# Low parts of 216 split weight blocks: ScalarE negation and an accumulating DMA instead of a VectorE subtraction

## The chip, the cores and the metric

One Trainium2 chip, one of its cores. The metric is the device time of one execution in microseconds (us). The kernel before has a median of 2792.41 us over 3 runs (2788.8 to 2797.22).

## The reference, cut to what matters

One decoder layer over 2048 tokens of 1024 channels, in float32. A conditioning vector gives a shift, a scale and a gate for each of the two halves of the layer:

```
h = rmsnorm(x) * (1 + sc_mix) + sh_mix
proj = h @ w_in                       # 1024 x 4624, split into z, xbc, dt, glu_a, glu_b
y = gated_rmsnorm(ssd_chunked(silu(causal_dwconv(xbc, 4 taps)), dt) + skip, z)
u = silu(layernorm(causal_dwconv(glu_a * sigmoid(glu_b), 31 taps)))
x = x + g_mix * (concat(y, u) @ w_out)             # 2048 x 1024
h = rmsnorm(x) * (1 + sc_mlp) + sh_mlp
x = x + g_mlp * (square(relu(h @ w_mlp1)) @ w_mlp2)
out = rmsnorm(x)
```

## The kernel before, in words

Channels lie on the 128 partitions, tokens on the free axis. The sequence is worked in two halves of 1024 tokens, each as two quarters (`qq`) of 512, which is the width of one matmul's result.

**Two-part operands.** A float32 product is made from two reduced-precision parts of each operand: the high part is a copy in the type float32r, the low part is the raw value minus the high part. Of a product three matmuls are made: high weight with high activation, high weight with low activation, low weight with high activation. For each slice `k` of a weight block they stand in this order (lines 303, 304 and 305 in the input projection, 846 to 848 in the output projection, 1085 to 1087 in the second MLP product), so the low part of a block is first wanted by its third matmul.

**Weight blocks.** `split_w` (line 288) fetches one block of 128 x 1024 float32 (512 KB): SyncE issues the load into `wr` (line 290, a ring of 3 buffers, shared with the loads of `m_d`, of `w1` and of `hid_d`), ScalarE copies it to the high part `wh` (line 293, a ring of 2), VectorE subtracts to make the low part `wl` (line 294, a ring of 2). These two run under `urgent()`, which gives them the first priority when the order of each engine's instructions is laid down. `split_w` is called 216 times: 72 blocks of the input projection (`w_in`), 64 of the output projection (`w_out`), 80 of the second MLP product (`w2`). Eight of the calls name their own destination (`big` buffers), the first four of these at the very start; 208 use `wh` and `wl`.

**How long one block serves.** In the input projection a block serves both quarters: 2 x 8 slices x 3 = 48 matmuls. In `mix_q` (output projection, called four times, 16 blocks each) a block serves one quarter: 24 matmuls. In `down` (second MLP product, called twice) the first three of four rounds use 48 matmuls a block (line 1117, 2 x 24 blocks), the last round 24 (line 1136, 2 x 16 blocks).

**Order of the stages in the span:** input projection with the SSD chunks, half 0 (0 to about 520 us) and half 1 (to about 1018); output projection of half 0 (1018 to about 1195); first MLP product of half 0 (`up`, to about 1530, which uses `w1` and not `split_w`); `down` of half 0 (to about 2030), whose last round is interleaved by blocks with the output projection of half 1 (to about 2100); `up` of half 1 (to about 2390); `down` of half 1 (to the end).

**Work beside it.** VectorE also makes the 31-tap convolution (`conv_cf`, lines 368 to 391: gather of `u_d` into `cu`, some 45 steps a tile, stores to `v_d`), put far back in priority, so that it fills gaps. The convolution of half 1 runs from about 1050 us. The layer norm over it (`ln_cf`, lines 400 to 429) gathers `v_d` into `cu`, sums with a matmul (line 410) and stores to `m_d`. In the input projection each of 12 convolution blocks a half (`conv_ssd`) has two small GpSimd copies a quarter (`halo`, lines 656 and 658) between ScalarE's evacuation (657) and VectorE's taps (662).

**GpSimd's queue.** GpSimd executes in order and issues these transfers: loads of `w_ada` (177), `u_d` (354, 368, 390 and 391 for `v_d`), 400 and 429 of the layer norm, stores of `x2_d` (920, each behind the evacuation 851), stores of `hid_d` (1059, behind ScalarE's line 1004) and loads of `hid_d` (1076, 64 of them, into the `wr` ring). The order on every engine's queue is laid down when the kernel is built.

The lines that hold the split:

```python
        raw = t_wr()
        nc.sync.dma_start(raw, src)
        hi, lo = dst or (t_turn("wh", 2, [P, D], F32R), t_turn("wl", 2, [P, D], F32R))
        with urgent():
            A.activation(hi, raw, AF.Copy)
            V.tensor_tensor(lo, raw, f(hi), SUB)
```

Of the kernel before, what the change touches and what calls it, by code (L numbers as in the profile page):

```python
# [9 lines left out]
F32R = mybir.dt.float32r  # L10
AF = mybir.ActivationFunctionType
ALU = mybir.AluOpType
MULT, ADD, SUB, MAX, MIN = ALU.mult, ALU.add, ALU.subtract, ALU.max, ALU.min

P = 128
S = 2048
D = 1024
# [29 lines left out]
def tile_layer(ctx, tc, x, w_ada, w_mod, vecs, w_in, w_dt, w_out, w1, w2, out):  # L47
    nc = tc.nc
    V, A, G, T = nc.vector, nc.scalar, nc.gpsimd, nc.tensor
# [12 lines left out]
    def nm(s):  # L62
        count[0] += 1
        return f"{s}{count[0]}"
# [4 lines left out]
    def t_turn(tag, n, shape, dt=F32):  # L69
        i = turns.get(tag, 0)  # L70
        turns[tag] = i + 1
        return cp.tile(shape, dt, tag=f"{tag}{i % n}", name=nm(f"{tag}{i % n}_"))
# [66 lines left out]
    @contextmanager  # L139
    def urgent():  # L140
        a = tc.cur_priority
        tc.cur_priority = 0
        yield
        tc.cur_priority = a + 1

    def f(ap):
        return ap.bitcast(F32)
# [137 lines left out]
    def t_wr():  # L285
        return t_turn("wr", 3, [P, D])

    def split_w(src, dst=None):
        raw = t_wr()
        nc.sync.dma_start(raw, src)  # L290
        hi, lo = dst or (t_turn("wh", 2, [P, D], F32R), t_turn("wl", 2, [P, D], F32R))
        with urgent():
            A.activation(hi, raw, AF.Copy)  # L293
            V.tensor_tensor(lo, raw, f(hi), SUB)  # L294
        return hi, lo


# [196 lines left out]
    for half in range(2):  # L494
        pre = {}
        if half == 0:
# [5 lines left out]
            for sg in range(4):  # L502
                wts.append([d_wm().rearrange("p (a b) -> p a b", a=2) for _ in range(4)])
                for j in range(4):
                    nc.sync.dma_start(wts[sg][j], w_mod[sg, j])
                held[W0[sg]] = split_w(w_in[W0[sg]], (d_bx(F32R), d_bx(F32R)))
# [54 lines left out]
            for n, b in enumerate(W1):  # L561
                held[b] = split_w(w_in[b])
                pre[b] = [t_mm()]
                block_mm(pre[b][0], held[b], hq0)
                if n == 0:
                    rs1 = bcast(rs1)
                    hq1 = []
                    for k in range(KT):
                        V.tensor_tensor(x1[k], x1[k], rs1, MULT)
                        hq1.append(lead_h(x1[k], k, d_hq[1](F32R)))  # L570
            hq = [hq0, hq1]
        else:
            held = {b: split_w(w_in[b]) for b in W0[:2]}
            hq = [hq0]
            pre["dt"] = [t_bm()]
# [656 lines left out]
```

## Time and profile before

| what | value |
|---|---|
| median of 3 runs | 2792.41 us (2788.8 to 2797.22) |
| the profiled execution, its own time | 2800.03 us |
| its span, first to last instruction | 2798.2 us |
| mean granted TensorE clock | 0.981 |
| bytes moved | 367.94 MB, mean 131 GB/s |

PE is TensorE's matmul side, PEld its weight load, DVE is VectorE, ACT is ScalarE, POOL is GpSimd, SP is SyncE; a q behind a name is the engine's instruction queue. Matmuls are pipelined, so the 0.39 us of one matmul row overlaps the next one's; the distance from start to start is what a matmul costs. A line number is that of the kernel's file.

### The profile page before, as it was taken

The page shows a single profiled execution, that of the slowest core. Times are in us where ns is not written, and L with a number is a line of the kernel's source. Part 1 is how long each engine was busy: PE and PEld are TensorE (multiplying, and loading weights), DVE is VectorE, ACT ScalarE, POOL GpSimd, SP SyncE. Part 2 cuts the span into 40 slices and gives each one's busy share as a digit, 9 for nine tenths or more (in the row PEclk, how much of TensorE's full clock was granted, in tenths as well). Part 3 has the DMA queues.
Part 4 walks back from the last instruction along what each step waited for, and adds up shares of the span by engine and source line. Part 5 has one row for each costly group of instructions (what it writes and reads, how often), then busy time and mean ns, then how long its engine had stood idle before and what let it go on. Part 6 is the DMA issues. An engine that isn't in the chain of part 4 may idle for free. (4 is left out here: it accounts for less than half of the span.)

```text
span 2798.2 us, 33574 instructions
## 1 busy us (share of the span) xinstructions
PE 2699.3 (96%) x12652; PEld 2195.9 (78%) x12652; DVE 2005.0 (72%) x3024; ACT 1360.2 (49%) x2065; POOL 273.3 (10%) x421
## 2 busy tenths in 40 slices
PE   7999999999999999979999899999998999999998
PEld 5778878788887788857887787888886888788886
DVE  7889999989986669999999755355457444433335
ACT  4757445586745664455565333242336555511222
POOL 2320210030030000000111110000000000100000
PEclk9999999999999999989999999999998999999999
DMA  7463224223223456413435543346632323623322
GB/s 286 141 197 114 84 85 134 77 92 111 85 91 106 136 189 214 140 61 128 142 129 176 179 144 121 97 146 208 203 116 87 113 98 121 223 91 100 106 83 106
DMA packets 115556, 367.94 MB, mean 131 GB/s; under 512 B 13376, under 2 KB 22208, under 8 KB 115392
## 3 DMA queue, kind: packets, MB, share of 16 engines
q1 hardware_dynamic: 79552, 239.54, 25.6%
q0 software_dynamic: 35840, 126.24, 13.3%
q8 instruction: 99, 1.62, 0.2%
q14 instruction: 65, 0.53, 0.1%
HBM read 281.58 MB, written 84.15 MB: 131 GB/s over the span
## 5 line engine op out<-in xcount | busy, mean ns | idle before, releaser
L293 ACT ACTIVATE wh<-wr 128x1024 fp32r<-128x1024 f32 x208 | 219.6, 1056 | 518.4 <-PE mm L1086 297.2
L303 PE MATMUL mm<-big,wh 128*128 128x512 f32 x1024 | 413.0, 403 | 4.1 <-DVE tp L708 3.6
L305 PE MATMUL mm<-big,wl 128*128 128x512 f32 x1024 | 404.4, 395 | 0.0
L1085 PE MATMUL mm<-big,wh 128*128 128x512 f32 x1024 | 401.9, 392 | 1.1 <-ACT wh L293 1.1
L304 PE MATMUL mm<-big,wh 128*128 128x512 f32 x1024 | 401.3, 392 | 0.0
L1087 PE MATMUL mm<-big,wl 128*128 128x512 f32 x1024 | 400.7, 392 | 0.6 <-DVE wl L294 0.5
L1086 PE MATMUL mm<-big,wh 128*128 128x512 f32 x1024 | 400.0, 391 | 0.0
L294 DVE TENSOR_TENSOR wl<-wr,wh 128x1024 fp32r<-128x1024 f32 x208 | 254.0, 1221 | 82.1 <-ACT wh L293 68.5
L1091 DVE SCALAR_TENSOR_TENSOR tp<-mm,gate,tp 128x512 f32<-128x512 f32 x128 | 95.3, 749 | 226.7 <-PE mm L1087 226.3
L303 PEld LDWEIGHTS mm<-big,wh 128*128 128x128 f32 x1024 | 193.1, 189 | 54.0 <-issue 9.2
L305 PEld LDWEIGHTS mm<-big,wl 128*128 128x128 f32 x1024 | 192.7, 188 | 43.8 <-issue 3.2
L304 PEld LDWEIGHTS mm<-big,wh 128*128 128x128 f32 x1024 | 193.2, 189 | 43.1 <-issue 4.7
L1087 PEld LDWEIGHTS mm<-big,wl 128*128 128x128 f32 x1024 | 193.2, 189 | 42.0 <-DVE wl L294 1.4
L1085 PEld LDWEIGHTS mm<-big,wh 128*128 128x128 f32 x1024 | 193.3, 189 | 41.6 <-ACT wh L293 1.9
L1086 PEld LDWEIGHTS mm<-big,wh 128*128 128x128 f32 x1024 | 193.2, 189 | 40.0
L848 PE MATMUL mm<-big,wl 128*128 128x512 f32 x512 | 199.8, 390 | 0.7 <-DVE wl L294 0.5
L846 PE MATMUL mm<-big,wh 128*128 128x512 f32 x512 | 200.0, 391 | 0.4 <-ACT wh L293 0.4
L847 PE MATMUL mm<-big,wh 128*128 128x512 f32 x512 | 199.3, 389 | 0.0
L383 DVE SCALAR_TENSOR_TENSOR ca<-cu,vec,ca 128x512 f32<-128x512 f32 x240 | 178.7, 744 | 1.1 <-ACT ca L377 0.9
L386 DVE SCALAR_TENSOR_TENSOR ca<-ca,hsum,ca 128x512 f32<-128x512 f32 x240 | 178.5, 744 | 0.0
L385 DVE SCALAR_TENSOR_TENSOR ca<-cu,vec,ca 128x513 f32<-128x513 f32 x224 | 167.4, 747 | 6.1 <-ACT ca L379 6.0
L878 DVE TENSOR_TENSOR big<-wr,big 128x1024 fp32r<-128x1024 f32 x64 | 77.7, 1222 | 120.3 <-ACT big L877 120.1
(281 smaller groups left out, 5289.9 us busy)
## 6 DMA issues: line engine op xcount, KB each, us to landing
wr<-in_w_dram SPq DMA_DIRECT2D x144, 512.0 KB, 3.4
wr<-in_w_in_dram SPq DMA_DIRECT2D x72, 512.0 KB, 3.5
wr<-in_w_out_dram SPq DMA_DIRECT2D x64, 512.0 KB, 4.1
hid_d<-tp POOLq DMA_DIRECT2D x64, 512.0 KB, 3.8
wr<-hid_d POOLq DMA_DIRECT2D x64, 512.0 KB, 3.9
ca<-in_w_ada_dram POOLq DMA_DIRECT2D x64, 256.0 KB, 3.6
tp<-ac_d SPq DMA_DIRECT2D x32, 512.0 KB, 4.3
wr<-m_d SPq DMA_DIRECT2D x32, 512.0 KB, 4.1
```

The costliest lines, as they stand in the source:

```text
L293: A.activation(hi, raw, AF.Copy)
L294: V.tensor_tensor(lo, raw, f(hi), SUB)
L303: T.matmul(ps, lhsT=hi[:, c], rhs=a[:, 0, :], start=(k == 0), stop=False)
L304: T.matmul(ps, lhsT=hi[:, c], rhs=a[:, 1, :], start=False, stop=False)
L305: T.matmul(ps, lhsT=lo[:, c], rhs=a[:, 0, :], start=False, stop=(k == KT - 1))
L383: V.scalar_tensor_tensor(a, x0[:, HP - i : HP - i + L], w(30 - 2 * i), a, MULT, ADD)
L846: T.matmul(ps, lhsT=hi[:, c], rhs=a[:, 0, :], start=(pos + k == 0), stop=False)
L847: T.matmul(ps, lhsT=hi[:, c], rhs=a[:, 1, :], start=False, stop=False)
L848: T.matmul(ps, lhsT=lo[:, c], rhs=a[:, 0, :], start=False, stop=(pos == 1 and k == KT - 1))
L1085: T.matmul(ps, lhsT=whl[0][:, c], rhs=hi, start=(k == 0), stop=False)
L1086: T.matmul(ps, lhsT=whl[0][:, c], rhs=lo, start=False, stop=False)
L1087: T.matmul(ps, lhsT=whl[1][:, c], rhs=hi, start=False, stop=(k == FB - 1))
```

## The change

The low part's buffer first gets minus the high part, by ScalarE; then GpSimd issues a DMA that reads the raw weights from device memory a second time and adds them to what lies in the buffer. The `wl` ring goes from 2 to 3 buffers. VectorE has no part in `split_w` any more. The line is in `split_w`, so that all 216 calls get it.

```diff
         raw = t_wr()
         nc.sync.dma_start(raw, src)
-        hi, lo = dst or (t_turn("wh", 2, [P, D], F32R), t_turn("wl", 2, [P, D], F32R))
+        hi, lo = dst or (t_turn("wh", 2, [P, D], F32R), t_turn("wl", 3, [P, D], F32R))
         with urgent():
             A.activation(hi, raw, AF.Copy)
-            V.tensor_tensor(lo, raw, f(hi), SUB)
+            A.activation(lo, f(hi), AF.Copy, scale=-1.0)
+            nc.gpsimd.dma_start(lo, src, accum_op=ADD)
         return hi, lo
```

## Rows read from the trace of the kernel before

**Rows 1.** The page: busy time of the engines; ScalarE's copy and VectorE's subtraction.
```profile
PE 2699.3 (96%) x12652; PEld 2195.9 (78%) x12652; DVE 2005.0 (72%) x3024; ACT 1360.2 (49%) x2065; POOL 273.3 (10%) x421
L293 ACT ACTIVATE wh<-wr 128x1024 fp32r<-128x1024 f32 x208 | 219.6, 1056 | 518.4 <-PE mm L1086 297.2
L294 DVE TENSOR_TENSOR wl<-wr,wh 128x1024 fp32r<-128x1024 f32 x208 | 254.0, 1221 | 82.1 <-ACT wh L293 68.5
```

**Rows 2.** Waits of PE (two) and ACT: total us, times, longest.
```profile
PE mm L1087 <- DVE wl L294: 0.5, 1, 0.5
PE mm L848 <- DVE wl L294: 0.5, 1, 0.5
ACT wh L293 <- PE mm L1086: 297.2, 55, 19.7
ACT wh L293 <- PE mm L847: 114.7, 36, 5.1
```

**Rows 3.** Busy time by stage: PE, PEld, DVE, ACT, POOL, clock, DMA share, GB/s.
```profile
1200.00:1300.00 100.00, 79.33 (x308) 60.10 (x307) 93.36 (x150) 55.17 (x96) 6.11 (x11) 0.85 0.26 90
1400.00:1500.00 100.00, 99.43 (x439) 81.97 (x438) 99.48 (x153) 57.68 (x98) 8.22 (x14) 1.00 0.35 119
1900.00:2000.00 100.00, 100.00 (x451) 83.08 (x450) 54.85 (x74) 34.58 (x46) 3.27 (x6) 1.00 0.71 235
10.00:45.00 35.00, 26.79 (x92) 14.64 (x91) 28.14 (x54) 14.70 (x23) 2.41 (x5) 0.90 1.03 407
```

**Rows 4.** Timeline, output projection of half 1: start, length, [idle before <- releaser].
```profile
2064.19 1.06 ACT L293 ACTIVATE wh<-wr 128x1024 fp32r<-128x1024 f32 x1 [4.33 <-PE mm L847]
2069.63 1.06 ACT L293 ACTIVATE wh<-wr 128x1024 fp32r<-128x1024 f32 x1 [4.38 <-PE mm L847]
```

**Rows 5.** Timeline, long blocks of `down`: ScalarE's copy, matmuls at a block boundary.
```profile
2648.91 1.06 ACT L293 ACTIVATE wh<-wr 128x1024 fp32r<-128x1024 f32 x1 [3.42 <-PE mm L1086]
2648.94 0.39 PE L1085 MATMUL mm<-big,wh 128*128 128x512 f32 x1
...
2649.39 0.39 PE L1087 MATMUL mm<-big,wl 128*128 128x512 f32 x1
...
2659.79 1.06 ACT L293 ACTIVATE wh<-wr 128x1024 fp32r<-128x1024 f32 x1 [9.82 <-PE mm L1086]
```

**Rows 6.** Timeline of `up`: two dependent ScalarE steps, the GpSimd store behind them.
```profile
2250.89 0.63 ACT L1003 ACTIVATE tp<-sp 128x512 f32<-128x512 f32 x1
2251.55 0.63 ACT L1004 ACTIVATE tp<-tp 128x512 f32<-128x512 f32 x1
2252.48 0.53 POOL L1059 DMA_DIRECT2D hid_d<-tp  x1 [16.03 <-ACT tp L1004]
```

**Rows 7.** GpSimd's 512 KB loads of line 1076: issue length, time from issue to landing.
```profile
L1076 POOL DMA_DIRECT2D wr<-hid_d x64: 528/528/554, 1492.8 to 2662.4; - x64
DMA to landing us min/median/max: 3.7/3.9/10.6
```

**Rows 8.** GpSimd's waits in the input projection, on VectorE: total us, times, longest.
```profile
POOL up L656 <- DVE big L662: 73.8, 24, 13.6
```

**Rows 9.** The chain that ended last, around 1590 us: start, length, what.
```profile
1584.09 0.77 DMA v_d<-ca
1587.80 3.94 DMA cu<-v_d
1593.70 1.22 PE bm L410 x2
```

**Rows 10.** One window of VectorE's line 294 alone: length, busy (count), clock, DMA.
```profile
1050.00:1584.00 534.00, 36.54 (x30) 0.97 0.44 147
```

**Rows 11.** Windows of PE alone: length, PE busy (matmuls), clock, DMA share, GB/s.
```profile
1205.00:1245.00 40.00, 23.19 (x73) 0.66 0.09 33
2100.00:2130.00 30.00, 18.60 (x57) 0.66 0.12 39
1584.00:1600.00 16.00, 9.16 (x28) 0.68 0.40 131
```

## The prediction

> **What bounds the kernel now.** I read the page's engine totals first: PE is busy 96% of the span, DVE 72%, ACT 49%, POOL 10% [rows 1]. So TensorE is the bound, and taking 254 us of DVE work away is worth only what PE waits for DVE. The list of waits says how much that is: all of PE's direct waits for the low part are 1.0 us [rows 2]. In the table by stage DVE is nearly full only from about 200 to 800 and 1000 to 1580 us, and PE beside it is at 99% in the row at 1400 [rows 3]; the exceptions are a dip at 1205 to 1245 and one at 1584 to 1600, where PE idles and the mean granted clock is 0.66 to 0.68, between its two levels of 1.0 (2.4 GHz) and 0.5 (1.2 GHz) [rows 11].
>
> Then the cycle of one weight block, from the timelines. ACT's copy to the high part almost always waits for PE: 55 and 36 waits, 297 and 115 us, on the last reader of the buffer [rows 2]. With two `wh` buffers, the high part of block n+2 starts when block n ends: 2648.91 against 2648.94 for the first matmul of the next block [rows 5]. A 48-matmul block lasts 10.88 us (2648.91 to 2659.79 [rows 5]); a 24-matmul block 5.44 us (2064.19 to 2069.63 [rows 4]). From that boundary the low part now takes 1.06 us on ACT and 1.22 on DVE [rows 1], 2.3 us, against 5.44 or 10.88 us of matmuls in between. It is covered everywhere.
>
> **The change part by part.**
>
> *DVE's subtraction goes:* 208 x 1.221 = 254 us of DVE [rows 1], plus 8 alike. PE waits 1.0 us for it. What can be won lies in the two dips. At 1584 PE waits for the convolution of half 1: the store lands, the gather takes 3.94 us, three DVE steps, then the sum on PE [rows 9]. From 1584 to 1600 PE ran 28 matmuls [rows 11] where, at 5.44 / 24 = 0.227 us each, 70 fit, so 42 x 0.227 = 10 us are lost. Between 1050 us, where this convolution starts, and 1584 stand 30 of the subtractions, 36.5 us of an almost full DVE [rows 10], so the convolution should end that much earlier and this wait goes. The dip at 1205 has 73 matmuls in 40 us, the same transition at 2100, with no convolution beside it, 57 in 30 us [rows 11]: 176 and 132 fit, so 103 x 0.227 = 23 us are lost against 75 x 0.227 = 17, so 6 us more can be had. Together 0 to -16 us; I take -12, since the order of the queues is laid down anew.
>
> *ACT's negation comes:* 216 x 1.06 = 229 us on an engine at 49% [rows 1], which goes to 57%. It delays the evacuation behind it by 1 us; the five PSUM buffers cover that, and I cost it at 0 (without that cover, 1 us a block).
>
> *The accumulating DMA comes:* 216 transfers of 512 KB, 113 MB more on 368. The new path from block boundary to finished low part is 1.06 (copy) + 0.03 (dependent ACT steps: 2250.89 + 0.63 to 2251.55) + 1.06 (negation) + 0.30 (ACT's end at 2252.18 to the POOL issue at 2252.48 [rows 6]) + D, so L = 2.45 + D, where D is issue to landing. No row shows an accumulating DMA. The nearest is the same size on the same queue without the addition, 3.7 at least, 3.9 median, 10.6 at most [rows 7]. An accumulate must read the buffer too: another 512 KB at the 407 GB/s that the full DMA engines reach [rows 3] is 1.3 us. I take D = 3.9 + 1.3 = 5.2, nearest to the median row, and keep 3.7 and 10.6 as bounds. L is then 7.65 us instead of 2.3.
>
> The Trainium skill, DMA: Bandwidth & Descriptors (section Anatomy of one DMA, the SWDGE path), fits a GpSimd transfer with about 2.0 us plus its bytes at 436 GB/s, an estimate of 3.2 us for 512 KB, by which no short block would stall and the first rival below would hold. The trace does not agree: even the plain copy never lands under 3.7 us [rows 7].
>
> *What that costs on short blocks.* Low n+2 is ready L after the end of block n. Block n+2 stops at its third matmul, 0.45 us in (2648.94 to 2649.39 [rows 5]), until then, and block n+1 fills one period p of that time. So two periods are L - 0.45 + 5.44, and p = (L + 4.99) / 2. A stall appears for L above 5.89 and half the excess is paid per block: (7.65 - 5.89) / 2 = 0.88 us. The 64 blocks of the output projection and 32 of the last rounds of `down` make 96 x 0.88 = +84 us. Bounds: D = 3.7 gives 0.13 x 96 = +12, D = 10.6 gives 3.58 x 96 = +344. A gain is excluded for this term: PE lost 1 us here before.
>
> *On long blocks* the limit is 10.88 + 0.45 = 11.3 us; L leaves 3.7 us. The third `wl` buffer lets ACT write before block n's low part is free, so it costs nothing. But POOL's queue is in order: the new issue waits for ACT, and stands behind `halo` copies that wait for ACT or DVE. Of these, 24 waits on DVE average 3.1 us, just inside the margin, and the longest is 13.6 [rows 8], 9.9 beyond it. I take +8, one such; bounds 0 and 24 x 9.9 = 238. Behind the waiting issue stand `hid_d` loads and `x2_d` stores, wanted many blocks later: 0.
>
> *At the start* the DMA engines are full, 407 GB/s from 10 to 45 us [rows 3]. Six early blocks add 3.1 MB, 7.7 us there; some of the loads are not awaited, so +4 (0 to 8; twice that if the second read counts fully). In 1900 to 2000, at 235 GB/s [rows 3], some 18 short blocks add 94 GB/s, twice that with the buffer's read: 423, slightly too much; the 4 us over are inside the bound of D.
>
> *SP* is relieved: `wr` is free after ACT's copy, 1.2 us earlier. Nothing waits on it more than now: 0.
>
> **Sum:** 84 + 8 + 4 - 12 = +84 us on the profiled execution's 2800.03 gives 2884. That execution is 7.6 above the median of 2792.41 (its span 2798.2 plus 1.8 around it), so 2876 for a median.
>
> **Rivals.**
>
> *Hidden, and DVE's relief counts.* With D near 3.7 the stalls are 12 us, the dips give 16, the rest nothing: 2788, no change. At D of 3.4 or less no stall is left: 2776. It decides at D = 3.8, where 96 x (D - 3.44) / 2 equals 16. For it: the plain copy lands at 3.7 at best. Against it: the median is 3.9 [rows 7], and that without a second read. This is the case on the other side: it is faster through the two dips, and D decides.
>
> *The accumulate is slow.* It may add at a lower rate than it reads, or queue behind other transfers: D = 8 is inside the spread of the plain copies [rows 7]. Then L = 10.45, the stall 2.28 x 96 = 219, and with that in place of the forecast's 84 the time is 3011; at 10.6 it is 3136. At D = 8 PE would idle for 30% of those stages; should the clock fall to half there, a block lasts 10.9 us, and the same L is covered, so the damage has a ceiling.
>
> *POOL's order.* Issues stuck behind instructions that wait for a late DVE, in the input projection: 24 waits beyond the margin by half of 9.9 us, 119 us on top, 2995. For it: POOL does wait there on DVE, 73.8 us in total [rows 8]. Against: behind a wait POOL may have had nothing else to do, the issue is urgent, and a relieved DVE is late less often.
>
> That DVE would not be relieved can't be: the instruction is gone from `split_w`.
>
> **Chances.** Forecast (slower, some 40 to 130 us) 0.50; hidden 0.22, of which faster 0.12 and same 0.10; slow accumulate 0.20; POOL's order 0.08. A measurement of this kernel can tell about 0.3%, 8.4 us, from no change. So faster 0.12, same 0.10, slower 0.78. The range takes in the forecast, most of the hidden case and half of the slow one: 2780 to 3060; the forecast's own is 2830 to 2930.
>
> **What the changed profile would show.** The subtraction's place taken by an ACT row of about 1.06 us, 208 times; DVE near 1750 us; a row of 216 accumulating issues on POOL whose landing time is D: right is 4.5 to 6, wrong below 4 or over 8. In PE's waits, the low-part matmuls of the output projection and of `down` should wait for that DMA by about 0.9 us a block in 1018 to 1195, in 1850 to 2100 and after 2690, and those of the input projection hardly at all. The wait at 1584 should be gone. I am wrong if the short blocks still have a 5.44 us pitch, or if the loss lies in the input projection.

## The result and the profile after

The changed kernel takes 3042.03 us (median of 4 runs, 3040.76 to 3047.01) against 2790.61 us for the kernel before on the same chip (4 runs, 2786.38 to 2797.22): ratio 1.0902, 95% interval 1.0876 to 1.0928, or 251 us slower. The forecast was slower by 84. The profiled execution's span is 3040.6 us, 242.4 longer than before.

The page of the changed kernel, engine totals and the costliest groups; every line behind 294 has moved down by one. [rows 1] and the first two of [rows 2] answer to them.

```profile
PE 2772.7 (91%) x12652; PEld 2228.2 (73%) x12652; DVE 1769.0 (58%) x2808; ACT 1568.7 (52%) x2277; POOL 438.0 (14%) x637
...
PEclk8999999999999989989999999999998999999999
...
L1088 PE MATMUL mm<-big,wl 128*128 128x512 f32 x1024 | 408.0, 399 | 48.6 <-DMA wl<-in_w_dram 48.4
...
L293 ACT ACTIVATE wh<-wr 128x1024 fp32r<-128x1024 f32 x208 | 219.7, 1056 | 621.5 <-PE mm L1087 355.6
L294 ACT ACTIVATE wl<-wh 128x1024 fp32r<-128x1024 f32 x208 | 218.7, 1052 | 2.7
L849 PE MATMUL mm<-big,wl 128*128 128x512 f32 x512 | 217.1, 425 | 95.2 <-DMA wl<-in_w_out_dram 95.1
```

VectorE lost 236 us of work and ScalarE gained 208, about as the parts said. But PE now waits 95.1 and 48.4 us for low parts, where it waited 1.0 [rows 2]. The number of matmuls is the same, yet PE is busy 73 us longer (2772.7 against 2699.3 [rows 1]): the same matmuls run at a lower clock (mean granted clock 0.959 against 0.981). The other 169 us of the longer span are PE's idle time, 3040.6 - 2772.7 = 268 against 2798.2 - 2699.3 = 99.

The accumulating issues of line 295: length of the issue on GpSimd (min/median/max), then the time from issue to landing.

```profile
L295 POOL DMA_DIRECT2D wl<-in_w_dram x80: 835/858/920, 1659.4 to 3013.9; - x80
L295 POOL DMA_DIRECT2D wl<-in_w_in_dram x64: 835/857/963, 67.7 to 1022.7; - x64
L295 POOL DMA_DIRECT2D wl<-in_w_out_dram x64: 835/852/936, 1059.4 to 2291.3; - x64
...
DMA to landing us min/median/max: 5.2/6.5/11.5
```

This is D, the term that no row of before showed: 6.5 us, above the 5.2 taken and inside the bounds of 3.7 and 10.6. The raw loads on SP's queue land nearly as before (medians 3.4 to 4.4 us).

The timeline of the changed kernel in the output projection of half 1, all short blocks: start, length, what, and in brackets the idle time before and its releaser.

```profile
2126.59 1.06 ACT L293 ACTIVATE wh<-wr 128x1024 fp32r<-128x1024 f32 x1 [0.52 <-PE mm L848]
2127.61 0.63 ACT L241 ACTIVATE sp<-tp 128x512 f32<-128x512 f32 x1
2128.14 1.04 ACT L294 ACTIVATE wl<-wh 128x1024 fp32r<-128x1024 f32 x1
...
2129.47 0.84 POOL L295 DMA_DIRECT2D wl<-in_w_out_dram  x1 [0.87 <-ACT wl L294]
...
2126.62 0.39 PE L847 MATMUL mm<-big,wh 128*128 128x512 f32 x1
...
2129.05 0.50 PE L849 MATMUL mm<-big,wl 128*128 128x512 f32 x1 [1.82 <-DMA wl<-in_w_out_dram]
2129.39 0.39 PE L847 MATMUL mm<-big,wh 128*128 128x512 f32 x1
...
2138.02 0.69 PE L849 MATMUL mm<-big,wl 128*128 128x512 f32 x1 [3.22 <-DMA wl<-in_w_out_dram]
2138.51 0.63 PE L847 MATMUL mm<-big,wh 128*128 128x512 f32 x1
2138.93 0.63 PE L848 MATMUL mm<-big,wh 128*128 128x512 f32 x1
...
2141.49 0.44 PE L848 MATMUL mm<-big,wh 128*128 128x512 f32 x1
2141.77 0.40 PE L849 MATMUL mm<-big,wl 128*128 128x512 f32 x1
```

At 2126.6 a high buffer has had its last reader (line 848); the copy starts at once, as in [rows 4]. Then another ScalarE step (line 241, a square) gets in front of the negation, GpSimd issues at 2129.47, and the third matmul that needs this low part starts at 2138.02: 11.4 us from the boundary, 8.5 of them the landing. The block in between had waited too, at 2129.05, for its own low part. After the wait at 2138 the matmuls follow at 0.43 us, nearly twice the 0.227 of [rows 4], from 2138.51 to 2141.49: the granted clock is at the lower of its two levels. Not every wait is followed by such a stretch. Of PE's 73 us more of busy time, 48 lie in the two output projections (22 and 26), which have 46 waits for low parts and, in the trace's clock record, 15 stretches at the lower level.

Windows of the changed kernel: length, busy time of PE, PEld, DVE, ACT, POOL (instructions), granted clock, DMA share, GB/s. They answer to [rows 3]; the first line is the kernel before in its output projection of half 0.

```profile
1019.00:1201.00 182.00, 180.73 (x816) 148.78 (x815) 172.49 (x261) 85.63 (x119) 15.70 (x25) 1.00 0.57 187
...
1100.00:1200.00 100.00, 73.96 (x286) 57.32 (x286) 66.47 (x101) 42.16 (x53) 17.41 (x23) 0.90 0.80 216
...
2100.00:2200.00 100.00, 78.54 (x305) 60.42 (x304) 21.24 (x31) 41.22 (x50) 15.63 (x21) 0.93 0.84 217
...
10.00:45.00 35.00, 22.58 (x65) 10.34 (x64) 21.68 (x45) 15.67 (x23) 3.39 (x6) 0.72 1.03 381
```

In these stretches of the two output projections PE is busy only 74 and 79% of the time, with the clock at 0.90 to 0.93, where it was full at 1.00 before. At the start, with the DMA engines as full as before, PE gets 4 us less done and the clock is 0.72 instead of 0.90.

Where the 242 us lie, by the first matmul of each stage, in us; the columns on the right are experiments told below (short: accumulation only in the 96 short blocks; long: in all others; input: only in the 64 ring blocks of the input projection; plain: all 216 transfers as plain copies; negation: no DMA, VectorE adds). By the lines of the matmuls, the stages follow one another: all of `down` of half 0, its last round of 16 short blocks too, lies before the output projection of half 1 (1549 to 1919 us and 1919 to 2097 in the kernel before), and is not interleaved with it as the kernel's description in words has it (in the changed kernel one block overlaps). The expectations call this output projection the stretch of last round and output projection of half 1.

| stage | before | after | short | long | input | plain | negation |
|---|---|---|---|---|---|---|---|
| input projection | 1019 | 1059 | 1018 | 1053 | 1057 | 1031 | 1017 |
| output projection, half 0 (32 short blocks) | 182 | 261 | 269 | 180 | 183 | 229 | 193 |
| `up`, half 0 | 348 | 339 | 340 | 344 | 343 | 340 | 346 |
| `down`, half 0 (24 long, 16 short) | 370 | 400 | 385 | 375 | 366 | 380 | 367 |
| output projection, half 1 (32 short) | 178 | 246 | 257 | 178 | 178 | 218 | 182 |
| `up`, half 1 | 334 | 333 | 334 | 335 | 334 | 335 | 335 |
| `down`, half 1 (24 long, 16 short) | 368 | 404 | 391 | 379 | 367 | 384 | 368 |

### The profile page after: what moved, and what is told of

Same layout as the page of the kernel before. It is cut to its first block, busy times and chain, and to the rows that moved or that the text cites. A ratio compares the mean times of both kernels' runs of the same rounds, so it can differ in the third digit from the quotient of the medians.

```text
span 3040.6 us, 34112 instructions
## 1 busy us (share of the span) xinstructions
PE 2772.7 (91%) x12652; PEld 2228.2 (73%) x12652; DVE 1769.0 (58%) x2808; ACT 1568.7 (52%) x2277; POOL 438.0 (14%) x637
## 4 chain that ended last, share of the span: by engine, by line
PE 38%; issue 30%; DMA 13%; DVE 10%; ACT 5%; POOL 3%; POOLq 0%; SPq 0%; DVEq 0%; ACTq 0%
PE mm L306 5%; PE mm L304 5%; PE mm L305 5%; PE mm L1031 4%; PE mm L1032 4%; PE mm L1033 3%; DMA wl<-in_w_out_dram 3%; PE mm L1088 2%; PE mm L1086 2%; PE mm L1087 2%; DMA tp<-ac_d 2%; POOL wl L295 2%; DMA wr<-hid_d 1%; DMA cu<-v_d 1%; DVE ca L384 1%
## 5 line engine op out<-in xcount | busy, mean ns | idle before, releaser
L1088 PE MATMUL mm<-big,wl 128*128 128x512 f32 x1024 | 408.0, 399 | 48.6 <-DMA wl<-in_w_dram 48.4
L304 PE MATMUL mm<-big,wh 128*128 128x512 f32 x1024 | 418.4, 409 | 2.3 <-DVE sp L671 2.2
L1086 PE MATMUL mm<-big,wh 128*128 128x512 f32 x1024 | 407.2, 398 | 7.9 <-ACT wh L293 7.9
L306 PE MATMUL mm<-big,wl 128*128 128x512 f32 x1024 | 404.8, 396 | 8.9 <-DMA wl<-in_w_in_dram 8.9
L1087 PE MATMUL mm<-big,wh 128*128 128x512 f32 x1024 | 404.3, 395 | 0.0
L305 PE MATMUL mm<-big,wh 128*128 128x512 f32 x1024 | 404.0, 394 | 0.0
L849 PE MATMUL mm<-big,wl 128*128 128x512 f32 x512 | 217.1, 425 | 95.2 <-DMA wl<-in_w_out_dram 95.1
L1088 PEld LDWEIGHTS mm<-big,wl 128*128 128x128 f32 x1024 | 196.0, 191 | 99.0 <-DMA wl<-in_w_dram 58.4
L306 PEld LDWEIGHTS mm<-big,wl 128*128 128x128 f32 x1024 | 194.8, 190 | 54.1 <-DMA wl<-in_w_in_dram 11.8
L1086 PEld LDWEIGHTS mm<-big,wh 128*128 128x128 f32 x1024 | 196.5, 192 | 49.6 <-ACT wh L293 9.6
L304 PEld LDWEIGHTS mm<-big,wh 128*128 128x128 f32 x1024 | 195.1, 191 | 50.3 <-issue 9.5
L305 PEld LDWEIGHTS mm<-big,wh 128*128 128x128 f32 x1024 | 194.9, 190 | 46.2 <-issue 7.1
L1087 PEld LDWEIGHTS mm<-big,wh 128*128 128x128 f32 x1024 | 196.0, 191 | 41.5
L294 ACT ACTIVATE wl<-wh 128x1024 fp32r<-128x1024 f32 x208 | 218.7, 1052 | 2.7
L847 PE MATMUL mm<-big,wh 128*128 128x512 f32 x512 | 212.3, 415 | 4.3 <-ACT wh L293 4.3
L848 PE MATMUL mm<-big,wh 128*128 128x512 f32 x512 | 210.6, 411 | 0.0
L849 PEld LDWEIGHTS mm<-big,wl 128*128 128x128 f32 x512 | 102.9, 201 | 136.7 <-DMA wl<-in_w_out_dram 115.4
```

What stands on the lines that cost most here:

```text
L294: A.activation(lo, f(hi), AF.Copy, scale=-1.0)
L304: T.matmul(ps, lhsT=hi[:, c], rhs=a[:, 0, :], start=(k == 0), stop=False)
L305: T.matmul(ps, lhsT=hi[:, c], rhs=a[:, 1, :], start=False, stop=False)
L306: T.matmul(ps, lhsT=lo[:, c], rhs=a[:, 0, :], start=False, stop=(k == KT - 1))
L847: T.matmul(ps, lhsT=hi[:, c], rhs=a[:, 0, :], start=(pos + k == 0), stop=False)
L848: T.matmul(ps, lhsT=hi[:, c], rhs=a[:, 1, :], start=False, stop=False)
```

## The experiments

The theory after the result: the chain from block boundary to finished low part is longer than the 5.89 us that a short block has for it (one block of 5.44 us and the 0.45 before the third matmul), mostly by D; half the excess is paid per block; the waits also cost clock. The rest is a smaller loss in the input projection and the long blocks.

**Where: the short blocks undone.** The 96 short blocks get VectorE's subtraction back:

```diff
+            if acc:
                 A.activation(lo, f(hi), AF.Copy, scale=-1.0)
                 nc.gpsimd.dma_start(lo, src, accum_op=ADD)
+            else:
+                V.tensor_tensor(lo, raw, f(hi), SUB)
...
-                        whl = split_w(ws[n])
+                        whl = split_w(ws[n], acc=False)
...
```

> Undoes the change in the 96 blocks that serve 24 matmuls only (64 of the output projection, 32 of the last rounds of the second MLP product): VectorE subtracts there again; the other 120 blocks keep the negation and the accumulating DMA. Theory (the loss is the late low part of short blocks, plus TensorE's clock falling after each such wait): the two output projection stretches go back from 260 and 246 us to 182 and 178, the last round of half 1 gives back some 30, so about 3042 - 78 - 68 - 35 = 2860, and the rest above 2791 lies in the input projection (40 us) and the long rounds. Rival (113 MB more traffic and GpSimd's full queue slow everything): 120 of 216 transfers stay, so over half of the 251 us stays, 2930 or more, and the output projection stretches get back at most half.

Measured 2853.44, ratio 1.0211 (1.0185 to 1.0237). The two output projections are back at 180 and 178 us. The theory holds: most of the loss is theirs. About 62 us are left. Its waits on the low parts of long blocks:

```profile
PE mm L1091 <- DMA wl<-in_w_dram: 13.1, 6, 6.5
```

**The other way round: only the short blocks accumulate** (the same flag, with the opposite values).

> The converse of the first run: the change only in the 96 blocks that serve 24 matmuls, VectorE's subtraction in the other 120. Theory (late low parts of short blocks are most of the loss, and the parts add up): 3042 - 2853 = 189 us of the loss belong to these blocks, so about 2792 + 189 = 2980; the input projection lasts 1019 us again, within 5. Rival (the parts feed one another, the long blocks' transfers delay the short ones'): under 2930.

Measured 2989.63, ratio 1.0709 (1.0688 to 1.0731): 197 us by the short blocks alone (2989.63 - 2792.98), and with the 62 of the run above (2853.44 - 2791.8) a little more than the whole 251. The landing of its accumulating DMAs:

```profile
DMA to landing us min/median/max: 5.1/6.3/10.7
```

And PE's waits on low parts in this run: total, times, longest.

```profile
PE mm L852 <- DMA wl<-in_w_out_dram: 107.3, 41, 6.7
PE mm L1091 <- DMA wl<-in_w_dram: 38.5, 18, 4.5
```

No other transfer makes low parts here, so the two rows are the whole direct wait of the short blocks: 145.8 us. The prediction's formula with D at 6.5 gives (2.45 + 6.5 - 5.89) / 2 x 96 = 147. The median of this run is 6.3, but a sum goes by the mean, which is 6.5 here: 6.8 for the 64 blocks of the output projections and 5.9 for the 32 of `down`. Taken apart, the formula gives 108 and 40 us, the rows show 107.3 and 38.5. PE stands still at about every second block (59 waits in 96 blocks) and then for the whole excess.

In PE's own time the 196 us of longer span are 132 us more idle time (the 145.8, less some other waits that went) and 64 us more busy time for the same matmuls (2763.0 against 2699.3), 59 of these in the two output projections. The first 183 us of the first of them, in this run (the kernel before is the first line of the windows above):

```profile
1018.00:1201.00 183.00, 137.46 (x532) 107.45 (x530) 113.71 (x188) 84.42 (x112) 30.34 (x39) 0.86 0.77 204
```

**How much of D is the addition.** A plain copy in place of the accumulation:

```diff
-            nc.gpsimd.dma_start(lo, src, accum_op=ADD)
+            nc.gpsimd.dma_start(lo, src)
```

> The same DMA without the addition: GpSimd copies the raw weights over the negated high part, so the low part holds the raw weights and the correction is left out of the low part's sum. Same bytes from device memory, same queue, same waits. Theory (issue to landing is 6.5 us because an accumulate reads the buffer, adds and writes): it falls to 3.9 to 4.4, L from about 9.4 to 7.1, the idle time per short block from 1.75 to 0.6 us, the total to 2880 to 2920. Rival (the transfer is late because of its queue and of the DMA engines' load): it stays over 5.5 us and the total over 3000.

Measured 2924.69, ratio 1.0472 (1.0445 to 1.0498), a little above the range given. The landing of the copies:

```profile
DMA to landing us min/median/max: 3.5/4.8/8.8
```

PE's waits on low parts with the plain copy:

```profile
PE mm L849 <- DMA wl<-in_w_out_dram: 55.6, 40, 5.7
PE mm L1088 <- DMA wl<-in_w_dram: 21.8, 23, 2.3
```

So the addition costs 1.7 us of landing, and the same transfer without it already takes 4.8 in these places, not the 3.9 of [rows 7]. The waits follow D: the formula gives 65 us at 4.8 and some 80 at the mean of 5.1, the rows 77, of which 4 belong to long blocks.

The 3.9 of [rows 7] did not come from other stages: 46 of those 64 loads stand in `down`, and in this run they land there in 3.9 again, beside plain copies that take 4.7. What goes with a late landing, in both traces, is company. Sorted by how many other transfers were in flight between 1.5 and 3.0 us after the issue, plain copies landed after 3.7 us (median) with none and 6.2 with three or more; accumulating transfers of the changed kernel after 5.4 (24 of the 208 into the ring) and 7.7 (57). So the addition costs about 1.5 to 1.7 either way, and the 5.2 that was taken is nearly the landing of a transfer that has the DMA engines to itself.

**A third high buffer, where memory allows.** A free buffer joins the ring of `wh` in the output projection of half 1, the last rounds and the second `down`:

```diff
+    def deep(on=True):
...
+        tag = ("wh0", "wh1", "cu0")[turns["deep"] % 3]
+        return t_at(tag, F32R), t_turn("wl", 3, [P, D], F32R)
...
-                        whl = split_w(ws[n])
+                        whl = split_w(ws[n], deep(q >= 2))
```

> Keeps the change in all blocks, but gives the high part a third buffer (a convolution buffer that is idle by then) in the output projection of half 1, in both last rounds of the second MLP product and in all of its half 1. Theory (a short block's period is set by copy, negation, issue and landing behind a ring of 2, (L + 5) / 2; with a ring of 3 it is (L + 5) / 3 = 4.8 us, under the 5.44 of its matmuls): the stretch of last round and output projection of half 1 goes from 246 to about 180 us, the last stage from 404 to about 372, in total about 3042 - 66 - 32 = 2945. Rival (the accumulating transfers themselves or GpSimd's queue cannot keep a pace of 5.44 us): both stretches stay within 15 us of what they are, total over 3010.

Measured 2992.58, ratio 1.0706 (1.068 to 1.0732): between the two expectations. The output projection of half 1 fell from 246 to 216 us, not to 180, and the second `down` from 404 to 383. So the gate on the high buffer is part of the path, but not all of what makes blocks late. In that output projection the transfers now land after 7.0 us instead of 6.2 (medians), with the DMA engines 85% busy instead of 77%: at the faster pace D itself is longer.

**Three high buffers everywhere, two low ones.**

```diff
-        hi, lo = dst or (t_turn("wh", 2, [P, D], F32R), t_turn("wl", 3, [P, D], F32R))
+        hi, lo = dst or (t_turn("wh", 3, [P, D], F32R), t_turn("wl", 2, [P, D], F32R))
```

> The changed kernel with three buffers for the high parts instead of two, and two for the low parts instead of three. The high part of block n+2 no longer waits for the end of block n; the negation still does, because its buffer is the one that block n's low part used. So the path from the block boundary to the finished low part loses the high copy and the step after it, 1.06 + 0.03 us: with the measured landing of 6.5 it is 7.86 instead of 8.95. Theory (half the excess over 5.89 is paid by each of 96 short blocks): (7.86 - 5.89) / 2 = 0.98 instead of 1.53 us a block, 53 us less waiting, and with the share of clock that such waits cost (197 us in all for 143 of waiting) about 70 less: 2970 to 2990. Rival: the buffers do not set the pace, ScalarE's order and the full DMA engines do; then the time stays above 3020. The lone third high buffer with three low ones gave 2993 in those stages where it could be had.

Measured 3088.28, ratio 1.1066 (1.1021 to 1.111): slower than the change, against the theory. The output projections took 253 us instead of 261 and 247 instead of 246; the input projection lost 21 us more and the first `down` 17. Its timeline on ScalarE and GpSimd in the first of these stages shows why nothing was won:

```profile
1218.61 1.06 ACT L293 ACTIVATE wh<-wr 128x1024 fp32r<-128x1024 f32 x1 [8.34 <-issue]
1219.58 1.04 ACT L294 ACTIVATE wl<-wh 128x1024 fp32r<-128x1024 f32 x1
...
1224.06 1.06 ACT L293 ACTIVATE wh<-wr 128x1024 fp32r<-128x1024 f32 x1 [2.92 <-issue]
1225.02 1.04 ACT L294 ACTIVATE wl<-wh 128x1024 fp32r<-128x1024 f32 x1
...
1226.36 0.87 POOL L295 DMA_DIRECT2D wl<-in_w_out_dram  x1 [0.33 <-DMA wl<-in_w_out_dram]
```

A negation still starts 1 us after a high copy. But here the two belong to different blocks: in this stage each negation starts 7.5 us (median) after its own copy, so the copy right in front is the next block's. With three high and two low buffers both wait for the same block boundary, and ScalarE runs the copy first. The path from the boundary is as long as before; only which block's copy lies on it has changed. Why the other stages became slower is not shown.

**Filling the wait with work.** Six matmuls with a zero weight in front of the third matmul of each short block, in the changed kernel and in the kernel before (the output projection's place; the one in `down` is alike):

```diff
+                        for _ in range(6 if k == 0 else 0):
+                            T.matmul(ps, lhsT=zero, rhs=a[:, 0, :], start=False, stop=False)
```

> The changed kernel with six more matmuls (a zero weight, 512 columns, 1.36 us in all) in each of the 96 short blocks, between its second and third matmul, that is in front of the wait for the low part. They add zero to the sum. Theory (a wait costs twice: its own time, and then some microseconds of matmuls at the lower clock level): the added matmuls fill most of the wait and keep TensorE from standing still, so the granted clock stays nearer 1.00 in these stretches, PE's busy time of the original matmuls falls by up to 60 us, and the total goes DOWN, by 20 to 70 us, to 2970 to 3020, although 96 x 1.36 = 131 us of matmuls were added. Rival (the clock matters little, the wait is all): the total stays within 10 us of 3042 or rises.

> The kernel before with the same six zero-weight matmuls in each short block, where nothing waits. It prices them: 96 x 6 x 0.227 = 131 us, total about 2922. In the changed kernel they cost 22 us, so 109 of 131 us would have gone into waits and regained clock. If instead they cost much less here (under 100), the run of the changed kernel says less about the waits than that.

Measured 3064.41 in the changed kernel, ratio 1.0972 (1.0934 to 1.1009), and 2916.25 in the one before, ratio 1.0445 (1.0418 to 1.0471). The first expectation failed: the time rose by 22 us and did not fall. The control was near its expectation, +123 us for 576 matmuls. So 101 of the 123 us went into time that the changed kernel had to wait or ran slowly in. Its direct waits on low parts fell from 143.5 to 60.9 us:

```profile
PE mm L854 <- DMA wl<-in_w_out_dram: 44.5, 28, 7.2
...
PE mm L1095 <- DMA wl<-in_w_dram: 16.4, 12, 2.6
```

PE's idle time fell by 83 us (267.9 to 184.9). Its busy time rose by 102 (2772.7 to 2874.5) where the control's rose by 119 (2699.3 to 2818.1), so about 17 us of clock came back. In this form it is less than the filling cost; another filling was not tried.

**The input projection alone.** Accumulation only in its 64 ring blocks, not in the eight with buffers of their own (the flag as above, and):

```diff
-            if acc:
+            if acc and dst is None:
```

> The change only in the 64 blocks of the input projection that use the wh and wl rings (48 matmuls each); subtraction in the 8 blocks with their own buffers, the first four at the start among them, and everywhere after. Theory: the start gives back 9 of the 34 us that the input projection lost in the first run (its DMA engines are full there), GpSimd's queue order keeps some 20 to 25: the input projection lasts about 1040, the total 2805 to 2815. Rival (a covered low part costs nothing and VectorE's relief counts): the input projection lasts 1019 or less, total 2775 to 2795.

Measured 2826.98, ratio 1.0123 (1.0105 to 1.0142), above both expectations. Leaving the eight early blocks out did give the start back (the stage's 288th weight matmul at 118 us, 120 before, 129 in the changed kernel), but by the 1152nd of 3456 it was as late as the changed kernel again (381 and 383 us, 362 before), and the stage still took 1057 us, 38 more than before. This loss is not at the start, and the sum had +4 and +8 where it lies. Its waits in PE's list:

```profile
PE mm L309 <- DMA wl<-in_w_in_dram: 12.5, 6, 3.9
...
PE bm L414 <- DVE ca L411: 9.1, 1, 9.1
```

**ScalarE or the transfers?** The negation stays in all 216 blocks, VectorE adds the raw weights; no new transfer:

```diff
-            nc.gpsimd.dma_start(lo, src, accum_op=ADD)
+            V.tensor_tensor(lo, raw, f(lo), ADD)
```

> ScalarE's negation as in the change in all 216 blocks, but the raw weights are added by VectorE from the raw buffer instead of by a DMA: no accumulating transfer, nothing of the change on GpSimd's queue, VectorE's work as before. The path from the block boundary is 1.06 + 0.03 + 1.06 + 1.22 = 3.4 us, under the 5.89 of a short block, so the short blocks lose nothing. What is left is the price of 229 us more on ScalarE. Theory (the loss of 34 to 40 us in the input projection comes from the transfers, their landing and the queue they stand in): at most 10 us in the input projection, 2795 to 2812 in all. Rival (it comes from ScalarE, whose other work, the state's and the modulation's steps, is 1.06 us later per block): the input projection takes 1045 us or more, 2820 to 2840 in all.

Measured 2810.89, ratio 1.0066 (1.0042 to 1.0089), inside the theory's range. The input projection takes 1017 us, as before: its loss comes with the transfers and not from ScalarE's extra work. The 17 us that remain lie in the two output projections (193 and 182 us). In the first of them VectorE is 91% busy, and an addition that waits for the negation comes late; the row of waits below is 6.7 of its 11 us. The window of that stage in this run, columns as above:

```profile
1019.00:1212.00 193.00, 185.25 (x820) 151.59 (x820) 175.75 (x263) 115.35 (x149) 15.64 (x25) 0.98 0.53 174
```

And from PE's list of waits:

```profile
PE mm L849 <- DVE wl L295: 6.7, 6, 2.2
```

**Which queue?** GpSimd's queue in the changed kernel, near the end of the input projection (timeline; L401 gathers for the layer norm, L430 stores its result):

```profile
951.19 0.85 POOL L295 DMA_DIRECT2D wl<-in_w_in_dram  x1 [13.98 <-ACT wl L294]
967.56 0.85 POOL L295 DMA_DIRECT2D wl<-in_w_in_dram  x1 [15.52 <-ACT bt L699]
981.60 0.80 POOL L430 DMA_DIRECT2D m_d<-cu  x1 [13.20 <-ACT cu L429]
984.74 0.86 POOL L295 DMA_DIRECT2D wl<-in_w_in_dram  x1 [2.34 <-ACT wl L294]
985.30 1.09 POOL L430 DMA_DIRECT2D m_d<-cu  x1
986.08 1.10 POOL L401 DMA_DIRECT2D cu<-v_d  x1
...
994.86 0.77 POOL L401 DMA_DIRECT2D cu<-v_d  x1 [4.15 <-DMA m_d<-cu]
...
995.75 0.69 DVE L405 TENSOR_TENSOR ca<-cu 128x512 f32<-128x512 f32 x1 [10.31 <-DMA cu<-v_d]
```

Accumulating issues stand 14 and 15.5 us at the head of the queue, waiting for ScalarE. The gathers go out at 986 and 995; VectorE waits 10.3 us for them, and PE 9.3 us for VectorE. In the kernel before the same two stores and two gathers stand at 946.03 to 955.52, so here they are 36 to 39 us later, in a stage that is 40 us longer as a whole. Three kernels tested whether this order makes the loss. In the first, the 64 loads of the modulation's weights also leave GpSimd's queue; the second is its control; in the third the gathers and stores of the layer norm move to SP's queue too:

```diff
-                nc.gpsimd.dma_start(wt, w_ada[k * P : (k + 1) * P, c0 : c0 + Q])
+                nc.sync.dma_start(wt, w_ada[k * P : (k + 1) * P, c0 : c0 + Q])
...
-            nc.gpsimd.dma_start(v, v_d[q // 2][:, 4 * j : 4 * j + 4, (q % 2) * 2 + i].rearrange("p k two n -> p k (two n)"))
+            nc.sync.dma_start(v, v_d[q // 2][:, 4 * j : 4 * j + 4, (q % 2) * 2 + i].rearrange("p k two n -> p k (two n)"))
...
-            nc.gpsimd.dma_start(m_d[q][:, KT + 4 * j : KT + 4 * j + 4, ts], vs[j])
+            nc.sync.dma_start(m_d[q][:, KT + 4 * j : KT + 4 * j + 4, ts], vs[j])
```

> Accumulating blocks in the input projection alone (its ring blocks), as in the run of 2827, and in addition the 64 loads of the modulation's weights, which wait for VectorE buffer by buffer, are issued from SP's queue instead of GpSimd's. Theory (order on GpSimd's queue: accumulates stand behind those loads and those loads behind accumulates, between 110 and 350 us): the 20 us lost there come back and the time is 2800 to 2812, if the control (the kernel before with those loads on SP) is within 5 us of the kernel before. Rival (the DMA engines, 75 to 85% busy between 110 and 210 us, and landings that are late for that): 2820 to 2835. If SP's own queue suffers from the loads, the control shows by how much, and the difference of the two runs counts: 5 to 15 us for the theory, 25 to 40 for the rival.

> Control: the kernel before with the 64 loads of the modulation's weights issued from SP's queue. Both theories: within 10 us of the kernel before, since only the place of issue differs; more than that would be raw weight loads that stand behind a load waiting for VectorE.

> The run of 2825 (accumulating blocks in the input projection alone, modulation loads on SP's queue), and in addition the gathers and stores of the convolution's normalisation are issued from SP's queue. Theory (GpSimd's in-order queue: an accumulate at its head waits up to 16 us for ScalarE's negation while those gathers stand behind it, and TensorE waits 9.7 us once, near 975 us, for what they feed): that wait shrinks to under 3 us and the time is 2808 to 2818. Rival (the normalisation is late for another reason, ScalarE or VectorE): the wait of about 9 us stays and the time is 2820 to 2832. In both, what remains above 2787 is late low parts (10 us) and the modulation's and state steps (about 10 us) with the clock after them.

Measured 2825.06, ratio 1.011 (1.0095 to 1.0125); the control 2786.64, ratio 0.9971 (0.996 to 0.9981); the third 2826.61, ratio 1.0099 (1.0079 to 1.012). The first lies 38 us above its control, so the rival holds: the modulation's loads are not what makes the loss. In the third, the wait near 975 us shrank, by less than the theory said, and the time did not change:

```profile
PE bm L414 <- DVE ca L411: 5.7, 1, 5.7
```

On SP the gather again stood behind a store that waited for ScalarE (store at 976.00, gather at 978.83). Moving it to another in-order queue did not free it. So the transfers cost the input projection 38 us. In the run with its ring blocks alone these are 26 us more idle time of PE (58.3 against 32.1) and 12 us more busy time for the same matmuls (998.7 against 986.9). Of the idle time, late low parts (10 to 13 us) and this one wait (9) are seen; the sharing of the rest among modulation and state steps stays open. One run told above bears on it: with 216 plain copies, issued in the same places of the same queue, the stage took 1031 us, 12 more than before and not 40. Most of the loss goes with the addition, whose landing takes 6.7 us in this stage where the plain copy takes 4.9 (medians), and not with the order of the queue.

The control is the only kernel of the study that is faster than both: 8 us under the kernel before, about as much as a measurement can tell.

**Traffic without dependence.** The kernel before, and beside each subtraction two accumulating transfers of 256 KB into a buffer that nobody reads:

```diff
             V.tensor_tensor(lo, raw, f(hi), SUB)
+            for j in range(2):
+                nc.gpsimd.dma_start(side[:, j * Q : (j + 1) * Q], src[:, j * Q : (j + 1) * Q], accum_op=ADD)
```

> The kernel before, subtraction and all, plus two accumulating DMAs of 256 KB a block from the same weights into a spare buffer that nobody reads. The same bytes and the same additions, but no matmul waits for them. Theory (the price is the latency, not the traffic): under 15 us over the kernel before, 2792 to 2807, nearly all of it at the start and from GpSimd's queue. Rival (113 MB more, read, added and written, slow the other transfers): 2830 or more, raw weight loads landing 1 us later or more.

Measured 3313.83, ratio 1.186 (1.1831 to 1.1889). As a test of traffic it is inconclusive: since they depended on nothing in their block, all 432 transfers were issued between 13 and 1190 us, each behind the landing of the one before in the same buffer, and the rest of GpSimd's queue stood behind them. The input projection took 1542 us; the later stages were unchanged. GpSimd's waits:

```profile
POOL side L299 <- DMA side<-in_w_dram: 265.4, 148, 7.9
POOL side L299 <- DMA side<-in_w_in_dram: 243.3, 128, 6.2
POOL side L299 <- DMA side<-in_w_out_dram: 203.0, 120, 4.6
```

## Why the prediction was wrong in size

**Sign, place and the formula of the stall were right.** Short blocks stall on the low part and half the excess over 5.89 us is paid per block: 145.8 us measured with the short blocks alone, 147 from the formula with the measured D. The time lies in the range, near its upper end, but in part by luck: that end was held for D = 8, and D is 6.5. The 3011 of that rival is near the measured time because other terms filled the gap: of the 167 us between forecast and result, 63 are D, some 50 came on top in the short blocks, mostly the clock, and some 60 are the other blocks, for which the sum had +8, +4 and -12.

**The step that failed first is D in the sum.** It was taken as 3.9 + 1.3 = 5.2; it is 6.5. Both parts were low: the plain copy of the same bytes lands in 4.8 in these places, beside the raw loads and the other transfers of its stage, and the addition costs 1.7. Each microsecond of D is 48 us, so 1.3 more turn 84 into 147. The accumulate was thus between the forecast and the rival with D at 8. The estimate by the Trainium skill (DMA: Bandwidth & Descriptors, Anatomy of one DMA), 3.2 us, is under even the fastest of GpSimd's plain copies here, 3.5.

**A term was missing.** The prediction used the clock only as a ceiling on the damage and put its cost at nothing. In fact many of the waits were followed by a stretch at the lower clock level, as at 2138 us: of the 197 us of the short blocks, 64 are the same matmuls running longer, with a granted clock of 0.88 and 0.91 in the two output projections, 1.00 before.

**Long blocks and GpSimd's order, +8.** The runs with long and input blocks and with input blocks alone differ by 26 us (2853.4 - 2827.0). By the table, 16 of them lie in `down` (375 and 379 against 370 and 368 before); for the eight early blocks no loss shows, the input projection takes 1053 us with them and 1057 without. PE's 13.1 us of waits for low parts in long blocks came in 6 waits. The longest, 6.5, is the first block of the first `down` (1585 us), behind `up`, which uses no split blocks; the 3.7 us of margin had been counted for a block behind others of its kind.

**Input projection, +4 and hardly any waits.** It lost 40 us in the changed kernel and 38 with its ring blocks alone. The prediction said it would be wrong if the loss lay here; about a sixth of it does. The rival on GpSimd's order put 119 us here; the queue does show waits (14 to 15.5 us at its head), but the tests of the queue did not give the time back, and plain copies in the same queue lost only 12. What each part of the 38 is worth stays open.

**ScalarE's negation, 0.** The run without a transfer is 17 us slower, in the short stages, though with VectorE's addition on the path too. In the input projection it costs nothing.

**VectorE's relief, -12.** `up` of half 0, which begins with the first dip, got 9 us shorter, and the wait of [rows 9], at the start of `down`, is gone. That this is the relief is not shown: the output projection before it lasts 79 us longer, and the convolution goes on in that time too; where VectorE keeps all its additions (negation) `up` is 2 us shorter, and where it is relieved in the input projection alone 5. And a wait of the same kind, 9.3 us, appeared near 1000 us, at the end of the input projection.

## What to carry to other kernels

A step that is moved from an engine to a DMA must be priced as latency against the time from the freed buffer to the first use, and with rings of two this is one block and the start of the next (5.44 + 0.45 us for a short block here). Here some 260 us of VectorE time (216 x 1.221), for which TensorE waited 1.0 us, were traded for a chain of 8.95 us with 5.89 us of room. When a transfer of the new kind is not in the trace, take the nearest row with as many other transfers in flight as the new one will meet, and by its mean, and add to the waits of TensorE the slower matmuls behind them (here 64 us of busy time to 146 of waiting). A deeper ring helps only if it takes away the wait that is last: with three high and two low buffers the next block's copy took the place of this block's.

## What was not expected of the hardware

An accumulating DMA of 512 KB from device memory lands after 6.5 us (median of 216), the plain copy at the same places after 4.8. Its issue holds GpSimd 0.85 us, the plain one 0.53. With no other transfer in flight the accumulating one took 5.4, with three or more 7.7. After a wait of 3.2 us TensorE ran eight matmuls at about half rate (2138.0 to 2141.5), after one of 1.8 us at 2129.05 none. Filling the waits with useless matmuls gave back 101 of the 123 us that those matmuls cost, so it was not worth its price.
